# A channel shuffle: two load and three store buffers instead of three and two, a shared first slot, issuers exchanged

## Chip, cores, metric

One core of one Trainium2 chip. The metric is the device time of one execution in microseconds (us), the median over several executions. The span in a profile is about 1.8 us shorter than the time of the same execution (314.7 against 316.46 for the kernel before). Ratios in this document are the mean time of one kernel's fast runs over that of the other's fast runs of the same rounds, so they are not quite the ratio of the medians quoted beside them. Intervals are 95%.

## The reference

```python
batch, h, w, c = 16, 64, 64, 256
groups = 8
x = x.reshape(batch, h, w, groups, c // groups)
x = x.transpose(0, 1, 2, 4, 3)
x = x.reshape(batch, h, w, c)
```

Each pixel's 256 float32 channels, seen as 8 x 32, are transposed to 32 x 8. Nothing is computed: 67.11 MB come in and 67.11 MB go out.

## The kernel before

Pieces of q pixels in each of 128 partitions are loaded, permuted by one VectorE copy, and stored. A pixel is 1 KB, so a size of 38 is 38 KB in each partition, 4,864 KB in all. Three load and two store buffers of 38 KB each.

```python
_SIZES = [4, 8, 16] + [38] * 12 + [28]
_IN_BUFS = 3
_OUT_BUFS = 2
# ... pools with bufs=_IN_BUFS and bufs=_OUT_BUFS ...
for q in _SIZES:
    in_tile = in_pool.tile([P, biggest * c], F32, name="in_tile")
    nc.sync.dma_start(out=in_tile[:, : q * c], in_=rows(x_flat, first, q))
    out_tile = out_pool.tile([P, biggest * c], F32, name="out_tile")
    nc.vector.tensor_copy(
        out=out_tile[:, : q * c].rearrange("p (i j g) -> p i j g", j=CPG, g=G),
        in_=in_tile[:, : q * c].rearrange("p (i g j) -> p i j g", g=G, j=CPG),
    )
    nc.scalar.dma_start(out=rows(out_flat, first, q), in_=out_tile[:, : q * c])
    first += P * q
```

Who waits: a load for the copy that last read its buffer (three pieces ago), a copy for its load and for the store that last used its output buffer (two pieces ago), a store for its copy.

## Time and profile before

| | before |
|---|---|
| time, median of 3 runs | 317.06 us |
| span of the profiled run | 314.7 us |
| VectorE busy | 119.2 us (38%) |
| both DMA queues, share of 16 engines' time | 49.8 + 49.4% |
| VectorE waiting for stores | 175.9 us |

The prediction below shows the page's shares, the stretches and the waits. In these lines DVE is VectorE, ACT ScalarE, SP SyncE and POOL GpSimd; a q behind a name means that the engine only issued or waited. A stretch gives its start and end, its length, the busy time (and number of instructions) of VectorE and of GpSimd, the clock of TensorE (unused here), and last the DMA share and GB/s. A packet is counted whole in the stretch in which it starts, so a short stretch can show a share above 1.00 and a rate above the sustained one. A wait gives the microseconds in all, how many times, and the longest. A line of DMA issues ends with the time from issue to landing.

What the prediction doesn't show is the chain that ended last, by line, and how the copies lie in time at the end. In the timeline a line gives start, duration, engine, line, what was copied, and in brackets the idle time before it with what ended it.

```profile
DMA out_dram<-out_tile 74%; DVE out_tile L49 20%; DMA in_tile<-in_x_dram 2%; SPq L47 0%; DVEq L49 0%
```
```profile
20.36 3.90 DVE L49 COPY out_tile<-in_tile 128x4096 f32<-128x4096 f32 x1 [11.75 <-DMA out_dram<-out_tile]
...
294.01 6.54 DVE L49 COPY out_tile<-in_tile 128x7168 f32<-128x7168 f32 x1 [5.95 <-DMA out_dram<-out_tile]
```

### The profile page before, as it was taken

To read this page: it belongs to the slowest core of one execution; us is meant where nothing else is said; L and a number is where in the kernel's file an instruction comes from. 1 tells how busy PE (TensorE), PEld (TensorE's weight loads), DVE (VectorE), ACT (ScalarE), POOL (GpSimd) and SP (SyncE) were. 2 spreads that over 40 slices of the span, in tenths; PEclk is the share of its full clock that TensorE was granted. 3 is DMA by queue.
4 is the path that set the end of the run, shared out by engine and by line. 5 is a ranking of instruction groups with operands and counts; after the bars stand their busy time and mean duration, and the time that the engine had idled before them with its cause. 6 is when DMAs were issued, how large, how long until landed. Compare 5 with 4: busy or idle time off the path is not lost.

```text
span 314.7 us, 133 instructions
## 1 busy us (share of the span) xinstructions
DVE 119.2 (38%) x16; POOL 0.2 (0%) x4
## 2 busy tenths in 40 slices
DVE  3040645505506407407308209109109019046620
POOL 0000000000000000000000000000000000000000
DMA  8999999999999999999999999999999999999997
GB/s 308 452 398 454 413 419 466 396 475 396 455 415 445 425 430 440 425 445 415 455 396 470 401 465 406 460 411 460 411 460 411 460 411 455 428 395 454 455 418 306
DMA packets 4608, 134.22 MB, mean 427 GB/s; under 512 B 512, under 2 KB 512, under 8 KB 768
## 3 DMA queue, kind: packets, MB, share of 16 engines
q1 hardware_dynamic: 2304, 67.11, 49.8%
q10 hardware_dynamic: 2304, 67.11, 49.4%
HBM read 67.11 MB, written 67.11 MB: 427 GB/s over the span
## 4 chain that ended last, share of the span: by engine, by line
DMA 75%; DVE 20%; issue 0%; SPq 0%; DVEq 0%
DMA out_dram<-out_tile 74%; DVE out_tile L49 20%; DMA in_tile<-in_x_dram 2%; SPq L47 0%; DVEq L49 0%
## 5 line engine op out<-in xcount | busy, mean ns | idle before, releaser
L49 DVE COPY out_tile<-in_tile 128x9728 f32<-128x9728 f32 (+4 forms) x16 | 119.2, 7449 | 181.4 <-DMA out_dram<-out_tile 175.9
L71 POOL MEMSET const-bfloat16-1.0<- 128x1 bf16 x1 | 0.1, 102 | 0.0
L71 POOL MEMSET const-uint8-127<- 128x1 uint8 x1 | 0.1, 102 | 0.0
L71 POOL MEMSET const-float32-1.0<- 128x1 f32 x1 | 0.1, 99 | 0.0
L71 POOL MEMSET const-float32-0.0<- 128x1 f32 x1 | 0.1, 98 | 0.2 <-issue 0.2
## 6 DMA issues: line engine op xcount, KB each, us to landing
in_tile<-in_x_dram SPq DMA_DIRECT2D x12, 4864.0 KB, 46.8
out_dram<-out_tile ACTq DMA_DIRECT2D x12, 4864.0 KB, 37.0
in_tile<-in_x_dram SPq DMA_DIRECT2D x1, 3584.0 KB, 43.8
out_dram<-out_tile ACTq DMA_DIRECT2D x1, 3584.0 KB, 13.3
in_tile<-in_x_dram SPq DMA_DIRECT2D x1, 2048.0 KB, 11.0
out_dram<-out_tile ACTq DMA_DIRECT2D x1, 2048.0 KB, 26.7
in_tile<-in_x_dram SPq DMA_DIRECT2D x1, 1024.0 KB, 5.4
out_dram<-out_tile ACTq DMA_DIRECT2D x1, 1024.0 KB, 25.8
```

What stands on the lines that cost most here:

```text
L49: nc.vector.tensor_copy(out=out_tile[:, : q * c].rearrange("p (i j g) -> p i j g", j=CPG, g=G), in_=in_tile[:, : q * c].rearrange("p (i g ...
L71: nc = _bacc.Bacc("TRN2", target_bir_lowering=False, num_devices=1)
```

## The change

The intent: the copies no longer wait for stores (three store buffers); two load buffers pay for it in memory; the three small pieces share the first slot, so that four loads can be issued at once; loads come from ScalarE and stores from SyncE.

```diff
-_SIZES = [4, 8, 16] + [38] * 12 + [28]
-_IN_BUFS = 3
-_OUT_BUFS = 2
+_SLOTS = [[4, 8, 16]] + [[38]] * 12 + [[28]]
+_IN_BUFS = 2
+_OUT_BUFS = 3
@@ the loop, cut
-    for q in _SIZES:
+    for parts in _SLOTS:
         in_tile = in_pool.tile([P, biggest * c], F32, name="in_tile")
-        nc.sync.dma_start(out=in_tile[:, : q * c], in_=rows(x_flat, first, q))
         out_tile = out_pool.tile([P, biggest * c], F32, name="out_tile")
+        # pieces: size, first row and columns of each part of the slot
+        for q, start, cols in pieces:
+            nc.scalar.dma_start(out=in_tile[:, cols], in_=rows(x_flat, start, q))
+        for q, start, cols in pieces:
+            nc.vector.tensor_copy(...)   # as before, on these columns
+            nc.sync.dma_start(out=rows(out_flat, start, q), in_=out_tile[:, cols])
-        nc.scalar.dma_start(out=rows(out_flat, first, q), in_=out_tile[:, : q * c])
```

More of the change, by code (lines that the diff above doesn't have):

```diff
@@ L29 @@
     assert G * CPG == c
-    assert sum(_SIZES) * P == b * h * w
-    biggest = max(_SIZES)
+    assert sum(map(sum, _SLOTS)) * P == b * h * w
+    biggest = max(map(sum, _SLOTS))
     x_flat = x.rearrange("b h w c -> (b h w c)")
@@ L44 @@
     first = 0
-    for q in _SIZES:
+    for parts in _SLOTS:
         in_tile = in_pool.tile([P, biggest * c], F32, name="in_tile")
-        nc.sync.dma_start(out=in_tile[:, : q * c], in_=rows(x_flat, first, q))
         out_tile = out_pool.tile([P, biggest * c], F32, name="out_tile")
-        nc.vector.tensor_copy(
-            out=out_tile[:, : q * c].rearrange("p (i j g) -> p i j g", j=CPG, g=G),
-            in_=in_tile[:, : q * c].rearrange("p (i g j) -> p i j g", g=G, j=CPG),
-        )
-        nc.scalar.dma_start(out=rows(out_flat, first, q), in_=out_tile[:, : q * c])
-        first += P * q
+        at = 0
+        pieces = []
+        for q in parts:
+            pieces.append((q, first, slice(at * c, (at + q) * c)))
+            first += P * q
+            at += q
+        for q, start, cols in pieces:
+            nc.scalar.dma_start(out=in_tile[:, cols], in_=rows(x_flat, start, q))
+        for q, start, cols in pieces:
+            nc.vector.tensor_copy(
+                out=out_tile[:, cols].rearrange("p (i j g) -> p i j g", j=CPG, g=G),
+                in_=in_tile[:, cols].rearrange("p (i g j) -> p i j g", g=G, j=CPG),
+            )
+            nc.sync.dma_start(
+                out=rows(out_flat, start, q), in_=out_tile[:, cols]
+            )
 _INS = ['x', 'groups']
```

## The prediction

> **What bounds the kernel now.** I read the page first: busy shares, the 40 slices, the queues.
>
> ```profile
> DVE 119.2 (38%) x16; POOL 0.2 (0%) x4
> DMA  8999999999999999999999999999999999999997
> GB/s 308 452 398 454 413 419 466 396 475 396 455 415 445 425 430 440 425 445 415 455 396 470 401 465 406 460 411 460 411 460 411 460 411 455 428 395 454 455 418 306
> q1 hardware_dynamic: 2304, 67.11, 49.8%
> q10 hardware_dynamic: 2304, 67.11, 49.4%
> ```
>
> The reader is to see that VectorE works 38% of the time, while the two DMA queues together fill 49.8 + 49.4 = 99.2% of the 16 engines' time. Next, the stretches view, cut at the first store packet (9.4 us), at the second large load (25.5), at the end of the loads (287) and at the last packet (313.5):
>
> ```profile
> 0.00:1.80 1.80, 0.00 (x0) 0.20 (x4) 1.00 0.10 16
> 1.80:9.40 7.60, 3.11 (x2) 0.00 (x0) 1.00 0.99 377
> 9.40:25.50 16.10, 3.90 (x1) 0.00 (x0) 1.00 1.02 433
> 25.50:287.00 261.50, 104.56 (x12) 0.00 (x0) 1.00 1.00 433
> 287.00:313.50 26.50, 7.61 (x2) 0.00 (x0) 1.00 0.97 420
> 313.50:314.70 1.20, 0.00 (x0) 0.00 (x0) 1.00 0.00 0
> ```
>
> The last two columns are the DMA share and GB/s. From 9.4 us to 287 us nothing is lost; what is not at full rate is 1.7 us ahead of the first packet, a load-only start at 377 GB/s, and 1.2 us after the last packet. Third, the waits of VectorE and the DMA issues, which at first sight tell another story:
>
> ```profile
> DVE out_tile L49 <- DMA out_dram<-out_tile: 175.9, 14, 14.6
> DVE out_tile L49 <- DMA in_tile<-in_x_dram: 5.5, 2, 4.1
> ```
> ```profile
> in_tile<-in_x_dram SPq DMA_DIRECT2D x12, 4864.0 KB, 46.8
> out_dram<-out_tile ACTq DMA_DIRECT2D x12, 4864.0 KB, 37.0
> ```
>
> VectorE waits 175.9 us for a store to free an output buffer, 14 times. The chain of waits says the same (74% of it is stores). That is the wait which the third store buffer removes. But it is a wait for the saturated engines, on an engine that isn't the bound. A 4,864 KB transfer alone takes 8 packets x 1.439 us = 11.5 us on each of the 16 engines; sharing them half and half it takes 23; it takes 37.0 from issue to landing because it first queues behind the previous store. So a store is always waiting in its queue, and a load (46.8 us) in the other.
>
> The packet records of the trace confirm the floor. Each of the 16 engines carries 8 packets (one per partition row) of each piece: 0.159 us for 4 KB, 0.309 for 8, 0.611 for 16, 1.439 for 38, 1.062 for 28 (medians). Sum per direction: 8 x (0.159 + 0.309 + 0.611 + 12 x 1.439 + 1.062) = 155.3 us; both directions 310.5; 32 semaphore packets of 0.009 add 0.3: 310.8 us. The first packet starts at 1.73 us, the last ends at 313.53 of the 314.7 us span, so 1.73 + 1.17 = 2.9 us lie outside. 310.8 + 2.9 = 313.7; the remaining 1.0 us is the start, where 16 KB loads take up to 1.07 us instead of 0.611.
>
> **What the Trainium skill says.** "DMA: Bandwidth & Descriptors", section "Queues, rings and completion order": each DMA engine takes turns between the queues it has work for, one packet at a time. The trace agrees: in steady state the 8 packets of a 38 KB load start over 20.2 us (60.63 to 80.84), that is 7 intervals of 2.89 us, two packets of 1.439 each. Same page, section "Issuing engines are not separate DMA queues": DMAs from ScalarE and SyncE run on the same 16 engines and interleave whoever issued them. Here both queues have 2304 packets and equal shares; a swap of the issuers is not tried in this trace. Same page, section "Where 436 GB/s comes from": a ceiling of 435.2 GB/s; the saturated stretches show 433, so there is nothing above to win. "Trainium Kernel Development and Optimization", section "Best Practices", asks for double buffering to overlap DMA with compute; whether two load buffers suffice depends on copy against transfer, worked out next.
>
> **The change part by part.** The same 16 loads, 16 copies and 16 stores with the same sizes remain, in the same order on each queue; the order listing of both programs shows only issuers and waits changed.
>
> 1. Issuers swapped. An issue takes 0.33 to 0.43 us on SyncE, 0.34 to 0.38 on ScalarE. Both leave the opening barrier together (0.650 and 0.655 us). On the path lies only the first load's issue: within 0.1 us of zero.
>
> 2. Shared first slot. 4, 8 and 16 KB and the first 38 KB load are issued at once, by about 2.2 us; before, the first 38 KB load was issued at 5.20. Its first packet started at 12.00, since three loads were ahead of it. Same packet: 0 us.
>
> 3. Third store buffer. The 16 KB copy waited until 20.36 us for the first store; now it runs when its load has landed, about 12.3 + 0.75 (semaphore packet to start of copy) = 13 us, done at 17. But its store cannot start before the 8 KB store is through: its first packet started at 33.78, and still will. Later copies start 14 us sooner, and their stores then wait 14 us longer in the queue: issue to landing 37 becomes about 51. Copies overlap saturated transfers: 0 us.
>
> 4. Two load buffers instead of three. Load n+2 is issued when copy n ends. Steady state: load n lands, the copy takes 8.80 us, issue to first packet about 1.0 us (0.73 to 1.73 at the start), so load n+2 is ready some 10 us after load n landed, while load n+1 occupies its queue for 23. Slack 13 us. An arriving queue does not get its turn at once: the first store was issued at 5.20, could start at about 6.2, started at 9.39, five 16 KB load packets later. I take five packets as already committed; with 1.439 us each that costs 7.2 us of the slack; 6 us remain. The tight place is the start: the first 38 KB load lands at about 25.6 + 0.7 = 26.3, copied by 35.2, next load ready at 36.2; the load ahead has its last packet start at 38.97. The margin is 2.8 us, less than five committed packets (three of 1.44 and two of 0.61 = 5.5 us). If that bites, a few store packets go earlier and the load later; stores are waiting, so the engines don't idle: 0 us.
>
> 5. The end. Loads end at 286-287.5, last landing about 288.2. The last copy then runs at once, 6.54 us, to 294.8, its store ready at 295.9; the store before it holds the queue until 305. Before, the last store was issued at 300.59 and was ready at 301.6. Slack grows from 3 us to 9, hidden: 0 us.
>
> Sum: 0 us, with some tenths either way from parts 1 and 2. Outside the span lie 317.06 - 314.7 = 2.4 us (another execution), unchanged.
>
> **The rivals.** (a) The removed store wait is real gain: 14 waits of up to 14.6 us go, the kernel gets several per cent faster. For it: the chain and the waits view. Against it: the floor of 310.8 us of packets. Even without the idle at both ends and the slow start, 310.8 + 2.4 = 313.2 us is 1.2% below 317.06, so a gain over 2% would need faster packets. (b) Two load buffers starve the load queue, a load wait takes the store wait's place, and loads and stores alternate with gaps. If nothing overlapped a copy, the 12 large copies would cost 12 x 8.8 = 106 us (423 us in all); if 1 us were lost per piece, 12 us (329). Against it: the 13 us slack, and a store backlog that keeps the engines fed when loads are late. (c) ScalarE issues loads late or the two queues are served unequally: for instance 0.3 us for the first packet and slower load-only packets, up to 2 us (319). Against: equal shares before. (d) An earlier rush of loads lengthens the slow load-only phase. Each extra 1 us of it costs 1 - 377/433 = 0.13 us: nothing.
>
> **Range and chances.** My figure is 317.0 us. The floor limits the gain; spread of repeated runs is about 0.1 us here, to which I add another chip or session and (c): 315.8 to 318.4. Chance of faster by over 2% (under 310.7, below the packets' own 310.8 with nothing else): 0.01. Slower by over 2% (over 323.4) needs over 6 us of new gaps in both queues: 0.02. Within: 0.97.
>
> **What would show it.** Right: DMA share 1.00 at 433 GB/s between 10 and 285 us; VectorE's waits turned from stores to loads, with a similar total (last copy's end minus busy time, 295 - 119 = 176 us), store issue to landing about 51 us and load about 37 (46.8 less up to 14, no longer issued as early); last copy ending near 295 instead of 300.55; its store's first packet still near 304. Wrong: a stretch under 430 GB/s in the middle (b), a first packet later than 2.0 us or unequal packet spacing (c), a last copy later than 301, which would leave a gap ahead of the last store, or 38 KB packets other than 1.439 us, which would move the floor itself.

## The result

| | before | after |
|---|---|---|
| time, median of 6 runs | 317.0 us (316.43 to 317.15) | 316.26 us (316.24 to 316.29) |
| ratio | | 0.9979, interval 0.9966 to 0.9992 |
| span of the profiled run | 314.7 us | 314.5 us |

Executions over 1.5% slower than the fastest of the same kernel are left out of the means. The time stayed within 2%, 0.2% lower. The profile after: busy shares, queues (number 10 is now the loads' queue, 1 the stores'), chain by line, waits, and DMA issues.

```profile
DVE 119.5 (38%) x16; POOL 0.2 (0%) x4
...
q10 hardware_dynamic: 2304, 67.11, 49.9%
q1 hardware_dynamic: 2304, 67.11, 49.4%
...
DMA in_tile<-in_x_dram 74%; DVE out_tile L57 19%; ACTq L55 0%; DVEq L57 0%
...
in_tile<-in_x_dram ACTq DMA_DIRECT2D x12, 4864.0 KB, 37.0
out_dram<-out_tile SPq DMA_DIRECT2D x12, 4864.0 KB, 49.8
```
```profile
DVE out_tile L57 <- DMA in_tile<-in_x_dram: 175.3, 16, 14.2
```

The wait for stores is gone altogether, and a wait for loads of the same size stands in its place: 175.9 us became 175.3. The chain was 74% stores and is 74% loads. Here, where one full resource feeds and drains VectorE, its idle time kept its size and only changed its name. A store now takes 49.8 us from issue to landing instead of 37.0: it is issued 12.8 us earlier and waits that much longer in its queue.

The same stretches as in the prediction's second fence (last two columns: DMA share, GB/s):

```profile
1.80:9.40 7.60, 3.16 (x2) 0.00 (x0) 1.00 0.99 387
9.40:25.50 16.10, 3.93 (x1) 0.00 (x0) 1.00 1.01 431
25.50:287.00 261.50, 105.73 (x12) 0.00 (x0) 1.00 1.00 433
287.00:313.50 26.50, 6.65 (x1) 0.00 (x0) 1.00 0.97 420
```

The middle, 261.5 us of the span, is the same to the last digit: share 1.00 at 433 GB/s. The timeline shows how much earlier the copies run without anything being gained:

```profile
12.64 3.93 DVE L57 COPY out_tile<-in_tile 128x4096 f32<-128x4096 f32 x1 [3.88 <-DMA in_tile<-in_x_dram]
...
288.15 6.65 DVE L57 COPY out_tile<-in_tile 128x7168 f32<-128x7168 f32 x1 [11.17 <-DMA in_tile<-in_x_dram]
```

The 16 KB copy starts at 12.64 us instead of 20.36, the last at 288.15 instead of 294.01. But in the packet records of the two traces the 16 KB store's first packet starts at 33.78 us before and at 33.65 after, and the last store's first packet at 304.41 and 304.40. The engines do the same packets at the same times, to within 0.2 us; only the slack in front of them (how long a store stands ready before its first packet) moved.

### The profile page after: what moved, and what is told of

Read it like the earlier page. It is cut to its first block, busy times and chain, and to the rows that moved or that the text cites. A ratio compares the mean times of both kernels' runs of the same rounds, so it can differ in the third digit from the quotient of the medians.

```text
span 314.5 us, 131 instructions
## 1 busy us (share of the span) xinstructions
DVE 119.5 (38%) x16; POOL 0.2 (0%) x4
## 4 chain that ended last, share of the span: by engine, by line
DMA 74%; DVE 19%; ACTq 0%; issue 0%; DVEq 0%
DMA in_tile<-in_x_dram 74%; DVE out_tile L57 19%; ACTq L55 0%; DVEq L57 0%
## 5 line engine op out<-in xcount | busy, mean ns | idle before, releaser
L57 DVE COPY out_tile<-in_tile 128x9728 f32<-128x9728 f32 (+4 forms) x16 | 119.5, 7467 | 175.3 <-DMA in_tile<-in_x_dram 175.3
## 6 DMA issues: line engine op xcount, KB each, us to landing
out_dram<-out_tile SPq DMA_DIRECT2D x12, 4864.0 KB, 49.8
```

What stands on the lines that cost most here:

```text
L57: nc.vector.tensor_copy(out=out_tile[:, cols].rearrange("p (i j g) -> p i j g", j=CPG, g=G), in_=in_tile[:, cols].rearrange("p (i g j) -> ...
```

## Experiments

Three theories were tried. **Theory:** both kernels are the same stream of packets; waits of copies are slack, and buffers count only when a queue runs empty. **Rival 1:** the 0.2% is a real gain of one part (issuers, or buffers). **Rival 2:** removing the store wait is worth something, and the smaller number of load buffers takes it back.

### The kernel before again, as a control

No edit.

> The kernel before, unchanged, as a control. Theory (both kernels are bound by the same packets, the 0.7 us is scatter of single executions): ratio 1.000 within 0.001, single times scattered from 316.4 to 317.2 us as in the earlier runs. Rival (the kernel before is really slower by some tenths for a reason in its own schedule): its times lie mostly at 316.9 to 317.2, never as tight as 316.24 to 316.29, and its profile shows a later first store or a longer start than the kernel after.

Measured: 316.49 us (316.27 to 316.94), ratio 0.9997 (0.9984 to 1.001) against 11 other executions of the same kernel, 316.22 to 317.43 us. So single executions of this kernel scatter over 1.2 us, more than the 0.74 us between the two medians of the result. The rival's "mostly at 316.9 to 317.2" did not come. Nor did a later first store or a longer start: its first store packet started at 9.11 us (9.19 in the kernel after), and the load-only stretch ran at 386 GB/s, against 377 in the first trace of this kernel and 387 in the kernel after.

The packet records show where the traced executions differ. Each of the 16 engines ends each transfer with a 4-byte semaphore packet (512 of them for 32 transfers). For the last store these lie, averaged over the engines, at 313.12 us in the kernel after, 313.11 before, 313.09 in this control, and 313.10 in each of the next two experiments. What differs is the last of the 16: 313.35, 313.53, 313.56, 313.38 and 313.24 us, in the same order. In the run with two store buffers below (317.60 us) 13 engines end by 313.26 us and three at 314.10 to 314.68. So the scatter of the traced runs is a few engines that end late, rather than more work; why they do is open. The slower executions of the result (316.9 to 317.2 us) have no trace, and the kernel after was not run again in another call, so its own scatter from call to call isn't known.

### Issuers alone

```diff
-nc.sync.dma_start(out=in_tile...)      # load
+nc.scalar.dma_start(out=in_tile...)
-nc.scalar.dma_start(out=rows(out...))  # store
+nc.sync.dma_start(out=rows(out...))
```

> Loads issued by ScalarE, stores by SyncE; three load and two store buffers as before. Theory: 316.2 to 317.1 us, ratio 0.998 to 1.001, VectorE still waits about 176 us for stores. Rival (the queue that carries the loads matters): it shows the whole 0.2% and times as tight as the kernel after (316.2 to 316.3).

Measured: 317.07 us (316.32 to 317.15), ratio 1.0004 (0.999 to 1.0019). VectorE waits 176.0 us for stores. The issuers give nothing, to within that interval; the rival falls.

### Buffers and shared slot alone

The kernel after with the issuers of before:

```diff
-nc.scalar.dma_start(out=in_tile[:, cols], ...)
+nc.sync.dma_start(out=in_tile[:, cols], ...)
-nc.sync.dma_start(out=rows(out_flat, start, q), ...)
+nc.scalar.dma_start(out=rows(out_flat, start, q), ...)
```

> Two load and three store buffers and the shared first slot; loads on SyncE, stores on ScalarE as before. Theory: 316.2 to 317.1 us, VectorE waits about 175 us for loads, last copy ends near 295 us. Rival (buffers give the 0.2%): ratio 0.998 with times near 316.3, and swap_only at 1.000.

Measured: 316.41 us, ratio 0.9993 (0.9979 to 1.0007); one execution of five, 336.21 us, is left out. VectorE waits 175.3 us for loads. The fast times, 316.24 to 316.74, are not as tight as those of the kernel after. Neither part reproduces the 0.2%, though the interval of this one would still allow it.

### Two store buffers instead of three

```diff
-_OUT_BUFS = 3
+_OUT_BUFS = 2
```

> The kernel after with two store buffers instead of three. Theory (a store is always waiting in its queue, so the third store buffer buys nothing): 316.2 to 317.1 us, VectorE's waits turn back to stores in part, last copy ends near 300 us, its store still starts near 304. Rival (the removed store wait was worth something that the two load buffers cost again): over 320 us.

Measured: 316.96 us (316.25 to 318.62), ratio 1.0011 (0.9988 to 1.0035). Its waits of VectorE:

```profile
DVE out_tile L57 <- DMA out_dram<-out_tile: 163.0, 12, 16.2
DVE out_tile L57 <- DMA in_tile<-in_x_dram: 19.4, 4, 9.7
```

163 us of waiting for stores are back, and the time is the same to within the interval (at most 0.35% longer; the kernel after itself wasn't among these rounds, so both are compared with the kernel before). The third store buffer buys nothing here beyond that. I had put the end of the last copy near 300 us; it came at 301.8 (295.14 + 6.68), and its store still started at 304.39.

### One store buffer

```diff
-_OUT_BUFS = 3
+_OUT_BUFS = 1
```

> The kernel after with one store buffer. A copy can then start only when the store before it has landed, so no store is queued during a copy. Theory: loads and stores fall into step, both end together, and the engines idle for a copy of 8.8 us and 1.0 + 0.75 us of issue and landing, 10.6 us for each of 12 large pieces and 8.3 us for the last: 12 x 10.6 + 8.3 = 135 us on top of 316, about 452 us (440 to 462); DVE waits for stores. Rival (loads fill the copy, stores fill the rest, no step is lost): near 317 us, at most 330.

Measured: 462.97 us (462.26 to 465.48), ratio 1.4631. The rival falls, and my 452 was 11 short. Two periods of its middle as stretches:

```profile
78.20:88.10 9.90, 8.82 (x1) 0.00 (x0) 1.00 0.00 0
88.10:112.80 24.70, 0.00 (x0) 0.00 (x0) 1.00 0.98 403
112.80:122.80 10.00, 8.80 (x1) 0.00 (x0) 1.00 0.00 0
122.80:147.10 24.30, 0.00 (x0) 0.00 (x0) 1.00 0.99 410
```

Copy and transfer alternate: DMA share 0.00 while VectorE copies, nothing on VectorE while the engines run. This is what a wait on the path looks like, against the 175 us of harmless waits above. The missing 11 us lie in the packet records. In 11 pieces the store's first 38 KB packet on each engine, after an empty spell, takes 2.27 us on average instead of 1.439, and the first packet of the load that follows it 1.64: about 1.0 us more in each, 11 us in all. The last two stores also start after an empty spell, but no load follows them, and their first packets take 1.455 us (38 KB) and 1.068 us (28 KB), nearly the usual time. So it isn't the empty spell alone; what makes these packets long isn't shown. Averaged over the engines, the empty spells are 136.0 us (135 expected) and longer packets 11.4 us more than in the kernel after: 316.3 + 136.0 + 11.4 = 463.7, against 463.63 in the profiled run.

### One load buffer

```diff
-_IN_BUFS = 2
+_IN_BUFS = 1
```

> The kernel after with one load buffer and three store buffers. Theory: the mirror of one store buffer; the next load is issued only when the copy is done, store and load run together, end together, and both queues are empty during the next copy; about 454 us (440 to 465), although three store buffers stand ready. Rival (three store buffers keep a backlog that fills the copies): under 335 us.

Measured: 472.12 us (468.84 to 473.19), ratio 1.4888, above my range. The mechanism is the expected one (share 0.00 during the copies, 403 GB/s between them):

```profile
105.30:115.30 10.00, 8.78 (x1) 0.00 (x0) 1.00 0.00 0
115.30:140.00 24.70, 0.00 (x0) 0.00 (x0) 1.00 0.98 403
```

Three store buffers do not help a load queue that runs dry: each side needs its second buffer. Here the first packets after the empty spell took 2.27 us (store) and 1.63 (load); the last store, behind which no load came, took 1.068 (28 KB). Averaged over the engines, the empty spells are 139.0 us and longer packets 13.5 us more than in the kernel after, which explains the profiled run (468.84 us): 316.3 + 139.0 + 13.5 = 468.8. Why the other three executions took 471.5 to 473.2 stays open; they have no trace.

### Each copy done twice, in both kernels

```diff
 nc.vector.tensor_copy(out=..., in_=...)
+nc.vector.tensor_copy(out=..., in_=...)   # the same copy again, same result
```

> The kernel after with each copy done twice into the same place (same result), 17.6 us instead of 8.8 for a large piece. Theory (the copy is hidden as long as copy and latencies stay under 23 us): nothing lost in the middle; at the end the last copy ends at about 287.6 + 0.7 + 13.1 = 301 to 307 us and the store before it runs out first, so a gap of about 3 us: 320 to 322 us. Rival (VectorE is on the path, as the chain of waits has it): 12 x 8.8 = 105 us more, about 420 us.

> The kernel before with each copy done twice. Theory: the copies wait for stores, the two last copies start late, and gaps of 8 and 1.6 us appear ahead of the last two stores (one 1.6 us gap at the start): about 327 us (324 to 330), so the changed buffers are worth about 2% here although they are worth nothing with the single copy. Rival (no difference in slack between the two kernels): the same time as after_copy_twice within 1 us.

Measured: after 321.82 us (321.54 to 323.42), ratio 1.0171 (1.0141 to 1.02); before 337.74 us (336.2 to 338.57), ratio 1.0656 (1.0618 to 1.0695). Doubling 119 us of VectorE work cost the kernel after 5 us, so the copies are hidden. And the two kernels, equal with single copies, are 4.5% apart with doubled ones (1.0171 / 1.0656 = 0.9545). A stretch of the middle and the end of each, the kernel after first:

```profile
108.00:132.00 24.00, 18.58 (x3) 0.00 (x0) 1.00 1.02 441
...
306.00:320.00 14.00, 3.03 (x1) 0.00 (x0) 1.00 0.63 268
```
```profile
108.00:132.00 24.00, 17.50 (x3) 0.00 (x0) 1.00 1.01 415
...
306.00:320.00 14.00, 13.97 (x3) 0.00 (x0) 1.00 0.52 222
320.00:336.00 16.00, 5.15 (x1) 0.00 (x0) 1.00 0.81 346
```

In the kernel after, a gap of 2.4 us lies ahead of the last store (the packets of the store before it end at 307.45 us, its own start at 309.89; averaged over the engines 2.9, where I had expected about 3). A gap of 0.6 us near 43 us, which I had not expected, and packets longer by 1.9 us than in the plain kernel after make up the rest of the 5 us. In the kernel before the gaps I had expected came: averaged over the engines 7.8 us ahead of the last store but one, 1.5 ahead of the last, 1.1 near 55 us, 10.4 in all. But it was 8 us over my range, and the rest is in the middle: share 1.01 and yet 415 GB/s. The engines are recorded as busy, with packets that last longer: a store's 38 KB packets took 1.56 to 1.61 us instead of 1.439, a piece 24.1 us instead of 23.0. Packets beyond their usual length make 12.3 us in this run against 1.4 in the plain kernel before: 10.9 more. 317 + 10.4 + 10.9 = 338. It isn't that the store queue runs empty between these pieces: the next store is issued about 6 us before the packets of the store ahead end (124.00 against 129.89 us), and its first packet comes 0.7 us after them (130.58), no later than in the kernel after with doubled copies (113.00 and 113.84), where packets keep their length. Why the packets of these stores are longer stays open.

### Doubled copies with two store buffers

```diff
-_OUT_BUFS = 3
+_OUT_BUFS = 2      # in the kernel after with doubled copies
```

> The kernel after with two store buffers instead of three and each copy done twice. The kernel before with doubled copies took 337.7 us and the kernel after 321.8 us; they differ in load buffers, store buffers, first slot and issuers. Theory A (the third store buffer made the 16 us): about 335 us, VectorE waiting for stores, DMA near 415 GB/s in the middle. Theory B (two load buffers and the shared first slot made it: loads cannot run further ahead than the stores follow, so the copies still wait for loads and a store is still queued when the last loads land): 321 to 324 us, 430 GB/s or more in the middle.

Measured: 322.04 us (321.91 to 322.73), ratio 1.0179. It ran on another chip than the two doubled kernels above, so it is compared by ratios: 1.0179 against 1.0171 and 1.0656. Its waits of VectorE show that the copies hardly ever needed a third store buffer:

```profile
DVE out_tile L57 <- DMA in_tile<-in_x_dram: 68.8, 15, 7.5
DVE out_tile L57 <- DMA out_dram<-out_tile: 0.9, 1, 0.9
```

Even with less slack, the third store buffer is worth nothing, and theory A falls. Of theory B this run confirms the time and the rate in the middle (426 to 441 GB/s); which of its two parts, the third load buffer or the small pieces in separate slots, costs the kernel before its 16 us was not separated, nor was the exchange of issuers tried with doubled copies.

### Loads alone and stores alone

Every load and one store, then one load and every store. Their outputs are wrong, which doesn't matter for the times.

```diff
 nc.scalar.dma_start(out=in_tile[:, : q * c], in_=rows(x_flat, first, q))   # 16 loads, 5 buffers
-nc.vector.tensor_copy(...)
-nc.sync.dma_start(out=rows(out_flat, ...), ...)                            # last piece only
```

> Wrong result on purpose: all 16 loads into five buffers, no copy, only the last piece stored. Theory 1 (loads alone are slower throughout, as in the first 9.4 us of both kernels at 377 to 387 GB/s): loads take 67.1 MB / 0.38 = 177 us, the whole about 191 us. Theory 2 (only the start is slow, by about 1 us): loads take 155.3 + 1 us, store 8.5, latencies 5 and 2 outside the span: about 171 us.

> Wrong result on purpose: one 38 KB load, then all 16 stores from that one tile. Stores alone run at the full rate in the last 20 us of both kernels: 1.7 + 11.5 + 2 + 155.3 + 1.2 + 1.8 = 173.5 us (172 to 175), packets of 38 KB at 1.439 us. If stores alone were slower: over 178 us.

Measured: loads 170.81 us, stores 174.66 us (two runs each). The first three stretches are of the loads, the last of the stores; VectorE has no column, as it did nothing.

```profile
1.80:9.40 7.60, 0.00 (x0) 1.00 1.01 409
9.40:25.50 16.10, 0.00 (x0) 1.00 1.05 454
25.50:150.00 124.50, 0.00 (x0) 1.00 1.00 430
```
```profile
25.50:150.00 124.50, 0.00 (x0) 1.00 1.00 430
```

Loads alone run at 430 GB/s after the start (theory 2), and stores alone too. The floor is nearly the same for loads alone, stores alone and both mixed: 1.440, 1.444 and 1.439 us for a 38 KB packet (medians). The slow start is a start-up cost of about a microsecond, not a lower rate of loads.

### A finer start

An attempt at a version that beats both:

```diff
-_SLOTS = [[4, 8, 16]] + [[38]] * 12 + [[28]]
+_SLOTS = [[1, 2, 3, 6, 16]] + [[38]] * 12 + [[28]]
```

> The kernel after with the first slot cut into 1, 2, 3, 6 and 16 KB instead of 4, 8 and 16. It tries to shorten the load-only start: the first store packet should start near 5 us instead of 9.2. Theory (a load-only us costs 1 - 387/433 = 0.11 us): 0.4 us less, 315.9 us, hardly above the scatter of single runs (316.2 to 317.4). Rival (small packets cost as much as they save): 316.3 us or more.

Measured: 321.95 us over six executions (318.87 to 324.71), ratio of the fast runs 1.0162 (1.0125 to 1.0198): 1.6% slower, clear of the scatter. The profiled run was the fastest of them, at 318.87:

```profile
1.80:9.40 7.60, 3.93 (x4) 0.00 (x0) 1.00 0.99 356
...
313.50:317.10 3.60, 0.00 (x0) 0.00 (x0) 1.00 0.04 16
```

The first store packet started at 7.38 us, not near 5, and the end has a stretch of 3.6 us with the engines almost empty (share 0.04). In the packet records the 16 engines drift apart early: the 16 KB store's semaphore packets are spread from 56.77 us (or earlier) to 67.34, and a copy that waits for the last of the engines waited 21.0 us there. By the next store they lie within 0.8 us again (78.03 to 78.84), but one engine stays behind: the last piece's semaphore packets come by 314.39 us on 15 engines and at 315.74 on one, where those of the kernel after lie between 312.87 and 313.35. The other fast runs, 319.3 to 323.4 us, have no trace, so their further 0.4 to 4.5 us are not explained (the run of 324.71 was slow).

## Why the prediction was right

- **The bound.** The packet floor held, in mechanism and not only in the number. The 38 KB packet stayed at 1.439 us in both traces, the middle at share 1.00 and 433 GB/s. This is the step that carried the prediction.
- **Part 1, issuers:** 0, shown alone (ratio 1.0004). The first packet starts at 1.74 us against 1.73. Rival (c) fell.
- **Part 2, shared slot** (read from the traces, not run alone): the first 38 KB load was issued at 2.10 us instead of 5.20; its first packet started at 11.92 against 12.00. 0, as worked out. The load-only stretch did not grow (387 GB/s against 377, the first store packet at 9.19 against 9.39), so rival (d) didn't come either.
- **Part 3, third store buffer:** 0, shown by taking it away again, with single copies (1.0011) and doubled ones. The 16 KB copy came at 12.64 us where 13 was worked out; store landing 49.8 where 51 was, as the later copies came 13 us sooner and not 14. Rival (a), the removed wait as gain, fell.
- **Part 4, two load buffers:** 0. The tight place that I named did not bite: the next load was issued at 34.81 and its first packet started at 40.93 us, 40.87 before. Rival (b) is true of one load buffer (1.4888), not of two.
- **Part 5, the end:** the last copy ended at 294.8 us (294.8 worked out), its store's packets started at 304.40; slack 8.6 us (9 worked out). With doubled copies the slack is used up: the gaps ahead of the last two stores make 9.3 us in the kernel before and 2.9 in the kernel after.
- **What it did not foresee:** the 0.2%. The interval excludes 1 in that comparison; the control scatters over more, and neither part alone shows it. I call it unsettled rather than a gain.
- **What it had wrong without harm:** the spread of repeated runs was put at 0.1 us, and executions of this kernel lay between 316.16 and 317.94; only what was added for another session made the range (315.8 to 318.4) wide enough. And 2.4 us outside the span came of two different executions; in one and the same it is 1.8 us (316.46 - 314.7), so the floor is 310.8 + 1.8 = 312.6 us and not 313.2. Neither touches the argument.

## What to carry to other kernels

A long wait in the chain is worth removing only if the resource it waits for has idle time; sum the packets first, add what lies outside, and compare with the span. Two buffers on each side were enough here, where a copy and its latencies (some 10.6 us) fit into the time that a piece occupies its queue (23 us); with one buffer on either side the kernel took 46 to 49% longer. What more slack is good for appears only when something gets slower, so test slack by doubling the hidden work.

## What the Trainium skill lacked or had wrong

- "DMA: Bandwidth & Descriptors", section "Queues, rings and completion order", lets an engine change queues at every packet, but says nothing of how long a newly filled queue waits for its first turn: the first store was issued at 5.20 us (5.19 after) and its first packet started at 9.39 (9.19), some five 16 KB load packets after it could have started. Nor has it a cost for restarting both queues after an empty spell: a store's first 38 KB packet then took 2.27 us and the following load's 1.64 where the others took 1.439, about 1 us for each piece; a store restarted alone took 1.455.
- The same page, section "Where 436 GB/s comes from", says that for transfers between HBM and SBUF the HBM side (about 358 GB/s) binds. Read alone this misleads for one running core: 433 GB/s were sustained for 261.5 us, and 430 by loads alone. The page's own measurement of a single core just above it (425 GB/s for 16 MB) agrees with the runs.
- "VectorE: DVE Perf Modes", section "The perf-mode tier table", gives 1227 ns for an fp32 copy of 2048 elements in SBUF. Here, where consecutive reads lie 32 elements apart, 2048 elements took 2025 ns; the table itself doesn't say for which access patterns it holds. That accesses far apart in SBUF are slower is said on another page, "SBUF — State Buffer", but without a figure for such a copy.
- No page says that many small packets at the start can set the 16 engines apart: with 1 to 6 KB pieces first, the semaphore packets of one store were spread over at least 10.6 us, and one engine ended the kernel 1.35 us after the other 15. What in the small pieces does it isn't shown.
